# A streaming-encoder block on one core: the first two down products of each feed-forward add into the residual in HBM

## The chip, the core and the metric

The kernel runs on one core of a Trainium2 chip. The core has a matrix engine (TensorE, PE in the profile, with its weight loads shown apart as PEld), three engines for elementwise work (VectorE or DVE, ScalarE or ACT, GpSimd or POOL), SyncE (SP), which here only issues transfers, and 16 DMA engines that move data between HBM, on-chip SBUF and so on. Products land in PSUM. Each engine works through its own list of instructions in order and waits on semaphores of the others. The metric is the device time of one execution in microseconds (us), the median of several runs; less is better.

## What is computed

One layer of an encoder block on x of 256 rows by 2048 columns, fp32: a half-step feed-forward, a mixer (pooling and gated linear attention), cross-attention to 256 memory tokens, a second half-step feed-forward, and a last norm.

```python
def swiglu(h, w_gate, w_up, w_down):
    return (jax.nn.silu(h @ w_gate) * (h @ w_up)) @ w_down
...
x = x + 0.5 * swiglu(rms_norm(x, ffn1_norm[l]), ffn1_w_gate[l], ffn1_w_up[l], ffn1_w_down[l])
...
x = x + jnp.concatenate([y_pool, y_gla], axis=-1) @ w_out[l]
x = x + mem_cross_attention(rms_norm(x, xattn_norm[l]), rms_norm(mem, mem_norm[l]),
                            xattn_w_q[l], xattn_w_kv[l], xattn_w_o[l])
x = x + 0.5 * swiglu(rms_norm(x, ffn2_norm[l]), ffn2_w_gate[l], ffn2_w_up[l], ffn2_w_down[l])
```

The inner width of the feed-forward is 5632. All weights, some 400 MB, are read once.

## The kernel before

**Products.** Each fp32 operand is split into a high and a low half of TensorE's own fp32 type, and a product is three matmuls (high by high, high by low, low by high) of 128x512 results. The weights come in units of 1 MB (`raw`, three buffers). ACT makes the high half `wh` by a cast, VectorE the low half `wl` by a subtraction. A plain unit is 24 matmuls. Some units are done with seven products in place of eight (`split_seven`, `seven`): VectorE first adds weight pieces into a tile `T`, both `T` and three pieces of `raw` are split (`wh`, `wl`, `xh`, `xl`), and the unit is 21 matmuls. Sums of the activations for such units are made once (`Sums`).

**Units and blocks.** `Stream` holds a list of units and of small operations between them, and emits them in order: a unit's weights are split two units ahead of its products, and its load is issued three units ahead of that split. A scheduler then sets the final order on each engine. `block_s` does one block of eight units for 1024 output columns in four PSUM tiles: two `whole` tiles that all units use, and two `parts` tiles that only the seven-product units use. When the last seven-product unit is done, `combine` (L579) turns the parts into an SBUF tile `e` (tag `sg`, two buffers): one copy on ACT and three sums on VectorE. At the block's end `join` (L593) finishes each half of 512 columns.

**Two ways to finish a block.** Gate and up blocks pass no `merge`: `join` has VectorE add the whole tile to `e` (L598), and both `combine` and `join` are marked `clump`, so that the last 768 of 2048 columns of the low half of the unit split just ahead go to GpSimd (`low_parts`, L459), which runs it beside VectorE's sums. Down blocks go through `into_x` (L834): the residual rows `x` (1024 columns, 256 rows, also tag `sg`) are fetched from HBM by SP, `early_parts` (L776) adds both halves of `e` to them as soon as the parts are combined (L781, twice), `residual` (L765) adds the two whole tiles at the block's end (L769, twice), and SP stores the rows to the HBM tiles `X[0]` and `X[1]` (L763). The factor 0.5 of the half-step is the scalar of these additions.

**Feed-forward.** `ffn` (L859) cuts the inner width into three parts of 2048, 2048 and 1536 columns (`FF_PARTS`). A part is gate and up blocks, then a down of two blocks, one for each `X[b]`. The first two downs take `WHOLE` (L825), eight units a block. The third down of the first feed-forward also turns the updated rows for the next norm; the third of the second feed-forward ends the kernel (`down_end`). The first down of the first feed-forward fetches its rows from the input x. `finish_norm` (L299) makes the factor `Rcol` of each row, which the gate uses in ACT's Silu (L874) and the up in VectorE's product (L882).

Of the kernel before, what the change touches and what calls it, by code (L numbers as in the profile page):

```python
# [8 lines left out]
F32R = mybir.dt.float32r  # L9
# [90 lines left out]
def build(ctx, tc, I, out):  # L100
# [68 lines left out]
    def ctl(name, shape):  # L169
        return whole_lines(const, shape, F32, name, name)  # L170
# [9 lines left out]
    gains = ctl("gains", [P, G_END])  # L180
    Rcol = ctl("Rcol", [P, 2])
    Rm = ctl("Rm", [P, 2])
# [116 lines left out]
    def finish_norm(n, spread_too=True):  # L299

        nc.vector.tensor_reduce(out=sums, in_=ss[:, :, :n], axis=AX.X, op=ALU.add)
        done = rsqrt(Rcol, sums, D, 2)
        if spread_too:
            diag["R"] = [diagonal(Rcol[:, t : t + 1]) for t in range(2)]
        return done
# [100 lines left out]
    class Sums:  # L406
# [8 lines left out]
        def make(self, g):  # L415
            act, i = self.act, self.pairs.index(g)
            n = 3 if self.over else 4
            if self.own and (i == 0 or i >= self.room):
                room, tag = (self.room, self.name) if i == 0 else (1, f"{self.name}{i}")
                t = scope["pool"].tile([P, room * 6 * P], F32R, tag=tag, name=uid(tag))  # L420
# [413 lines left out]
    def into_x(w, act, scale, gain=None, k0=0, nk=KT, spread_too=True, src=None, way=OUTPUT,  # L834
# [13 lines left out]
        if gain is not None:  # L848
            st.op(lambda: finish_norm(4, spread_too), way.folds[3] + 1)
            if spread_too:  # L850
                st.op(spread_norm, spread_at)

    FF_PARTS = ((0, 4), (4, 4), (8, 3))

# [4 lines left out]
    def ffn(wg, wu, wd, down, amid=None, end=None):  # L859
# [19 lines left out]
        def ev_up(j, c, held=gate):  # L879
            g = held[j]  # L880
            for h in range(2):
                nc.vector.scalar_tensor_tensor(  # L882
                    out=g[:, h, :], in0=c[:, h, :], scalar=Rcol[:, h : h + 1], in1=g[:, h, :],
                    op0=ALU.mult, op1=ALU.mult,
                )
# [55 lines left out]

    st.op(lambda: among_weights(first_factor), 6)
    st.op(more_gains, 14)
    st.op(lambda: turn_gains(G_MIX, G_END), 35)
# [7 lines left out]
    def down_first(wd, k0, nk, last, way):  # L952
        way.make_sums()
        if last:
            for g, after in zip(qk_sums.pairs[:2], (9, 11)):
                st.op(lambda g=g: among_weights(lambda: qk_sums.make(g)), after)
        into_x(wd, ys, 0.5, G_MIX if last else None, k0, nk, src=None if k0 else I["x"][0],
               way=way, spread_at=7)

# [543 lines left out]
    def down_last(wd, k0, nk, last, way):  # L1503
        if last:
            down_end(wd, k0, nk, way)
        else:
            way.make_sums()
            into_x(wd, ys, 0.5, None, k0, nk, way=way)

# [9 lines left out]
    def down_end(wd, k0, nk, way):  # L1519
# [45 lines left out]
        def update(nb, h):  # L1565
            xn = x_cols(nb * NB, NB)[:, h]
            return nc.vector.scalar_tensor_tensor(
                out=xn, in0=acc_ps[nb][:, h, :], scalar=0.5, in1=xn, op0=ALU.mult, op1=ALU.add
            )
# [6 lines left out]
        def last_update(i):  # L1576
            xn = x_cols(3 * NB, NB)[:, 1, columns(i)]
            return nc.vector.scalar_tensor_tensor(
                out=xn, in0=last_part(i), scalar=0.5, in1=xn, op0=ALU.mult, op1=ALU.add
            )  # L1580
# [98 lines left out]
        for b in range(2):  # L1679
            into = lambda j, ps: acc_ps.__setitem__(2 + j, ps)  # L1680
            block_s(wwide(wd, b * 2 * NB, k0, nk - 2), ys, way.sums, END_ORDER[b],
                    into if b else residual(0.5, 0, None), early_parts(0.5, b), (0,),
                    home=end_parts(b), more=b == 1)
# [78 lines left out]
```

## Time and profile before

| | |
|---|---|
| median of 3 runs | 2071.29 us (2071.0 to 2071.98) |
| span of the profiled execution | 2069.6 us |
| busy PE, DVE, ACT, POOL | 2059.1, 1843.7, 1173.7, 103.5 us |
| DMA, mean over the span | 211 GB/s, 435.92 MB |
| SP queue | 122840 packets, 434.12 MB |
| first down of the first feed-forward | 178.1 to 264.3 us, two blocks |

The profile gives no time of the profiled execution beside its span, so the span is set against the median of the runs, which is 1.7 us longer. A group of instructions is a line with its engine, operation, tile names (written tile, arrow, tiles read), shape, count, busy time, mean time of one in ns, and the idle time before it with what ended it. A row of the timeline begins with its start in us and its time. A matmul of 512 columns is shown with about 0.39 us, but the next one starts some 0.23 us after it, since they are pipelined; what counts for PE is the distance between starts.

### The profile page before, as it was taken

To read this page: it belongs to the slowest core of one execution; us is meant where nothing else is said; L and a number is where in the kernel's file an instruction comes from. 1 tells how busy PE (TensorE), PEld (TensorE's weight loads), DVE (VectorE), ACT (ScalarE), POOL (GpSimd) and SP (SyncE) were. 2 spreads that over 40 slices of the span, in tenths; PEclk is the share of its full clock that TensorE was granted. 3 is DMA by queue.
4 is the path that set the end of the run, shared out by engine and by line. 5 is a ranking of instruction groups with operands and counts; after the bars stand their busy time and mean duration, and the time that the engine had idled before them with its cause. 6 is when DMAs were issued, how large, how long until landed. Compare 5 with 4: busy or idle time off the path is not lost.

```text
span 2069.6 us, 24068 instructions
## 1 busy us (share of the span) xinstructions
PE 2059.1 (99%) x9464; PEld 1714.5 (83%) x9464; DVE 1843.7 (89%) x1720; ACT 1173.7 (57%) x1196; POOL 103.5 (5%) x93
## 2 busy tenths in 40 slices
PE   9999999999999999999999999999999999999998
PEld 7888888888888888888888888888888888888886
DVE  7998899989998779989889787989988999889987
ACT  7654455554554666665765544656554565545554
POOL 0000000000000000000000000000000010000001
PEclk9999999999999999999999999999999999999999
DMA  7666766566666655467655455666577765676664
GB/s 265 205 202 224 243 214 215 184 227 238 225 202 224 226 184 183 163 205 280 225 185 192 159 178 183 203 224 224 171 235 225 239 208 185 225 241 224 210 224 156
DMA packets 123129, 435.92 MB, mean 211 GB/s; under 512 B 9860, under 2 KB 13544, under 8 KB 122632
## 3 DMA queue, kind: packets, MB, share of 16 engines
q1 hardware_dynamic: 122840, 434.12, 62.9%
q8 instruction: 74, 1.21, 0.2%
q14 instruction: 39, 0.32, 0.0%
q10 hardware_dynamic: 176, 0.27, 0.0%
HBM read 417.58 MB, written 16.78 MB: 210 GB/s over the span
## 4 chain that ended last, share of the span: by engine, by line
PE 99%; DMA 0%; DVE 0%; SPq 0%; ACT 0%; POOL 0%; POOLq 0%; issue 0%; DVEq 0%
PE pt L362 64%; PE pt L509 30%; PE ph L791 2%; PE pl L1416 1%; PE pv L1453 1%; PE px L802 1%; PE pp L1049 0%; DMA x<-in_x 0%; PE pa L1077 0%; PE tm L1362 0%; PE po L1215 0%; PE px L728 0%; PE pq L1202 0%; PE pe L362 0%; PE pz L1093 0%; PE po L1218 0%
## 5 line engine op out<-in xcount | busy, mean ns | idle before, releaser
L362 PE MATMUL pt<-wh,xs 128*128 128x512 f32 x2432 | 780.8, 391 | 0.0
L1720 ACT CAST wh<-raw 128x2048 fp32r<-128x2048 f32 x242 | 461.7, 1912 | 228.9 <-PE pt L362 128.0
L455 DVE TENSOR_TENSOR wl<-raw,wh 128x2048 fp32r<-128x2048 f32 (+1 forms) x242 | 515.9, 2140 | 83.9 <-ACT wh L1720 83.7
L362 PEld LDWEIGHTS pt<-wh,xs 128*128 128x128 f32 x2432 | 455.9, 188 | 94.1 <-issue 0.5
L491 ACT CAST wh<-T 128x1024 fp32r<-128x1024 f32 x264 | 277.0, 1054 | 379.0 <-DVE T L488 362.4
L362 PE MATMUL pt<-wl,xs 128*128 128x512 f32 x1216 | 474.0, 390 | 0.0
L362 PE MATMUL pt<-wh,ys 128*128 128x512 f32 x1452 | 458.1, 389 | 0.0
L362 PEld LDWEIGHTS pt<-wh,ys 128*128 128x128 f32 x1452 | 272.5, 188 | 56.1
L455 DVE TENSOR_TENSOR wl<-T,wh 128x2048 fp32r<-128x2048 f32 (+1 forms) x132 | 296.7, 2248 | 5.6 <-ACT wh L491 5.2
L362 PE MATMUL pt<-wl,ys 128*128 128x512 f32 x726 | 283.0, 390 | 0.0
L362 PEld LDWEIGHTS pt<-wl,xs 128*128 128x128 f32 x1216 | 228.4, 188 | 46.2
L280 DVE TENSOR_TENSOR xl<-raw,xh 128x1536 fp32r<-128x1536 f32 x132 | 231.1, 1751 | 10.8 <-ACT xh L279 10.7
L279 ACT CAST xh<-raw 128x1536 fp32r<-128x1536 f32 x132 | 195.5, 1481 | 52.1 <-PE pt L509 30.7
L488 DVE TENSOR_TENSOR T<-T,raw 128x512 f32<-128x512 f32 x264 | 182.0, 690 | 6.8
L488 DVE TENSOR_TENSOR T<-raw 128x1024 f32<-128x1024 f32 x132 | 160.7, 1218 | 0.6
L362 PEld LDWEIGHTS pt<-wl,ys 128*128 128x128 f32 x726 | 136.3, 188 | 28.1
L509 PE MATMUL pt<-xh,xs 128*128 128x512 f32 x416 | 154.9, 389 | 0.0
L509 PE MATMUL pt<-wh,xs 128*128 128x512 f32 x396 | 153.9, 389 | 0.0
L459 POOL TENSOR_TENSOR wl<-raw,wh 128x768 fp32r<-128x768 f32 x44 | 81.6, 1854 | 1389.6 <-DVE wl L455 1366.8
L509 PE MATMUL pt<-wh,xe 128*128 128x512 f32 x320 | 124.3, 389 | 0.0
L509 PEld LDWEIGHTS pt<-xh,xs 128*128 128x128 f32 x416 | 78.1, 188 | 16.2
L509 PEld LDWEIGHTS pt<-wh,xs 128*128 128x128 f32 x396 | 74.3, 188 | 15.4
(274 smaller groups left out, 2081.4 us busy)
## 6 DMA issues: line engine op xcount, KB each, us to landing
raw<-in_ffn_w_down SPq DMA_DIRECT2D x88, 1024.0 KB, 5.5
raw<-in_ffn_w_up SPq DMA_DIRECT2D x80, 1024.0 KB, 5.0
raw<-in_ffn_w_gate SPq DMA_DIRECT2D x77, 1024.0 KB, 5.1
raw<-in_w_in SPq DMA_DIRECT2D x32, 1024.0 KB, 5.0
raw<-in_xattn_w_kv SPq DMA_DIRECT2D x32, 1024.0 KB, 5.0
raw<-in_w_out SPq DMA_DIRECT2D x16, 1024.0 KB, 6.7
raw<-in_xattn_w_q SPq DMA_DIRECT2D x16, 1024.0 KB, 6.2
raw<-in_xattn_w_o SPq DMA_DIRECT2D x16, 1024.0 KB, 5.7
```

The lines of the kernel that those rows point to most:

```text
L279: in_turn("scalar", lambda: nc.scalar.copy(hi, src))
L280: in_turn("vector", lambda: nc.vector.tensor_tensor(out=lo, in0=src, in1=f32(hi), op=ALU.subtract))
L362: latest["product"] = nc.tensor.matmul(ps, a, w, start=first and i == 0, stop=last and i == 2)
L455: in_turn("vector", lambda: nc.vector.tensor_tensor(out=lo[:, :n], in0=src[:, :n], in1=f32(hi[:, :n]), op=ALU.subtract))
L459: rest = nc.gpsimd.tensor_tensor(out=lo[:, n:], in0=src[:, n:], in1=f32(hi[:, n:]), op=ALU.subtract)
L488: in_turn("vector", lambda: nc.vector.tensor_tensor(out=o, in0=a, in1=b, op=ALU.add))
L491: in_turn("scalar", lambda: nc.scalar.copy(th[:, c], t[:, c]))
L509: nc.tensor.matmul(banks[n], x, w, start=n in fresh and j == 0, stop=n in ends and j == 2)
L791: rows["turned"] = nc.tensor.transpose(v[:, i, h * P : (h + 1) * P], g[:, h, i * P : (i + 1) * P], ident)
L802: nc.tensor.transpose(v[:, j, h * P : (h + 1) * P], x[:, h, j * P : (j + 1) * P], ident)
L1416: nc.tensor.matmul(ps[:, t, :M], ys[:, 4 * h + d, a, tok], xa["K", h][:, d, b, :], start=i == 0, stop=i == 11,)
L1720: in_turn("scalar", lambda: nc.scalar.copy(hi, raw))
```

## The change

In the first two downs of each feed-forward the residual rows are no longer fetched to SBUF, added to on VectorE and stored. `onto_x` takes the place of `into_x`: its blocks have no `merge`, so they finish like gate and up blocks (join into `e` on VectorE, both steps marked `clump`), and then GpSimd issues two transfers a block that add the joined 256 x 512 halves of `e` to `X[b]` in HBM. For the first down `X` must hold x already: eight transfers from HBM to HBM, issued by SP, copy the input (`copy_x`). The half-step's 0.5 moves into the up factor (`Rup`, one more VectorE instruction in each norm), and the additions of the third downs get 1.0. `Sums.make` names another home for sums past its first tile; no sums of this kernel lie past it. The products are the same.

```diff
-    Rcol = ctl("Rcol", [P, 2])
+    factors = ctl("Rcol", [P, 4])
+    Rcol, Rup = factors[:, :2], factors[:, 2:]
...
-        done = rsqrt(Rcol, sums, D, 2)
+        rsqrt(Rcol, sums, D, 2)
+        done = nc.vector.tensor_scalar_mul(Rup, Rcol, 0.5)
...
+    def copy_x(i):
+
+        b, rows_i = i % 2, slice(i // 2 * S // 4, (i // 2 + 1) * S // 4)
+        nc.sync.dma_start(X[b][rows_i, :], I["x"][0][rows_i, b * 2 * NB : (b + 1) * 2 * NB])
+
+    def added_to_x(b):
+
+        def evict(j, e):
+            nc.gpsimd.dma_start(
+                X[b][:, j * NB : (j + 1) * NB].rearrange("(h p) n -> p h n", p=P), e,
+                accum_op=ALU.add,
+            )
+        return evict
+
+    def onto_x(w, act, k0, nk, way):
+
+        for b in range(2):
+            block_s(wwide(w, b * 2 * NB, k0, nk), act, way.sums, way.orders[b], added_to_x(b),
+                    sevens=way.sevens[b])
...
-                    out=g[:, h, :], in0=c[:, h, :], scalar=Rcol[:, h : h + 1], in1=g[:, h, :],
+                    out=g[:, h, :], in0=c[:, h, :], scalar=Rup[:, h : h + 1], in1=g[:, h, :],
...
+    for i in range(8):
+        st.op(lambda i=i: copy_x(i), 15 + 2 * i)
...
-        if last:
-            for g, after in zip(qk_sums.pairs[:2], (9, 11)):
-                st.op(lambda g=g: among_weights(lambda: qk_sums.make(g)), after)
-        into_x(wd, ys, 0.5, G_MIX if last else None, k0, nk, src=None if k0 else I["x"][0],
-               way=way, spread_at=7)
+        if not last:
+            onto_x(wd, ys, k0, nk, way)
+            return
+        for g, after in zip(qk_sums.pairs[:2], (9, 11)):
+            st.op(lambda g=g: among_weights(lambda: qk_sums.make(g)), after)
+        into_x(wd, ys, 1.0, G_MIX, k0, nk, way=way, spread_at=7)
...
-            into_x(wd, ys, 0.5, None, k0, nk, way=way)
+            onto_x(wd, ys, k0, nk, way)
```

The built programs show where the scheduler put these steps. In the rows below the line number is that of each kernel's own file, a number behind a tile's name tells its buffers apart, and nothing tells of times.

SP's list at the start, from the last column of gains to the loads of the weights of the first gate block (`raw_219` is the fifth load of the kernel). Before:

```order
L685 DMA gain_787<-in_gla_b_a 4x128
L638 DMA raw_219<-in_ffn_w_gate 128x2x1024
L638 DMA raw_228<-in_ffn_w_gate 128x2x1024
L638 DMA raw_283<-in_ffn_w_gate 128x2x1024
L638 DMA raw_336<-in_ffn_w_gate 128x2x1024
```

Now:

```order
L689 DMA gain_788<-in_gla_b_a 4x128
L860 DMA X_105<-in_x 64x1024
L860 DMA X_106<-in_x 64x1024
L642 DMA raw_219<-in_ffn_w_gate 128x2x1024
L860 DMA X_105<-in_x 64x1024
L860 DMA X_106<-in_x 64x1024
L860 DMA X_105<-in_x 64x1024
L860 DMA X_106<-in_x 64x1024
L642 DMA raw_228<-in_ffn_w_gate 128x2x1024
L860 DMA X_105<-in_x 64x1024
L860 DMA X_106<-in_x 64x1024
L642 DMA raw_283<-in_ffn_w_gate 128x2x1024
```

The code asks for the copies from the 15th unit on, but they wait for nothing, and the scheduler moved them up: two stand ahead of the fifth load, six ahead of the sixth and eight ahead of the seventh.

ACT's list where the first gate block ends and the first up block (the ninth load, `wh_505` before, `wh_506` now) begins; `sg_583<-pt_174` and `sg_584<-pt_174` are the Silu of the first gate bank. Before:

```order
L279 CAST xh_507<-raw_389 128x1536
L285 CAST xs<-j_494 128x128
L285 CAST xe_268<-j_494 128x384
L491 CAST wh_505<-T_504 128x1024 x2
L1720 CAST wh_543<-raw_395 128x2048
L874 ACTIVATE sg_583<-pt_174,Rcol 128x512 x2
```

Now:

```order
L280 CAST xh_508<-raw_389 128x1536
L286 CAST xs<-j_495 128x128
L286 CAST xe_268<-j_495 128x384
L495 CAST wh_506<-T_505 128x1024
L898 ACTIVATE sg_584<-pt_174,Rcol 128x512 x2
L495 CAST wh_506<-T_505 128x1024
L1747 CAST wh_544<-raw_395 128x2048
```

The Silu of the first bank now stands between the two casts of that load's high half.

VectorE's list where the first block of the first down ends (about 214 to 235 us in the profile). Before:

```order
L455 TENSOR_TENSOR wl_1701<-raw_1596,wh_1700 128x2048
L584 TENSOR_TENSOR sg_1727<-pt_1637,sg_1727 128x512
L585 TENSOR_TENSOR sg_1727<-pt_1638,sg_1727 128x1024
L455 TENSOR_TENSOR wl_1735<-raw_1635,wh_1734 128x2048
L488 TENSOR_TENSOR T_1768<-raw_1674 128x1024
L588 TENSOR_TENSOR sg_1727<-pt_1638,sg_1727 128x512
L781 SCALAR_TENSOR_TENSOR x_1547<-sg_1727,x_1547 128x2x512
L488 TENSOR_TENSOR T_1768<-T_1768,raw_1674 128x512
L781 SCALAR_TENSOR_TENSOR x_1547<-sg_1727,x_1547 128x2x512
L769 SCALAR_TENSOR_TENSOR x_1547<-pt_1458,x_1547 128x2x512
L488 TENSOR_TENSOR T_1768<-T_1768,raw_1674 128x512
L280 TENSOR_TENSOR xl_1772<-raw_1674,xh_1771 128x1536
```

Now:

```order
L459 TENSOR_TENSOR wl_1706<-raw_1601,wh_1705 128x1280
L588 TENSOR_TENSOR sg_1733<-pt_1642,sg_1733 128x512
L589 TENSOR_TENSOR sg_1733<-pt_1643,sg_1733 128x1024
L592 TENSOR_TENSOR sg_1733<-pt_1643,sg_1733 128x512
L459 TENSOR_TENSOR wl_1739<-raw_1640,wh_1738 128x1280
L602 TENSOR_TENSOR sg_1733<-pt_1466,sg_1733 128x1024
L602 TENSOR_TENSOR sg_1733<-pt_1467,sg_1733 128x1024
L492 TENSOR_TENSOR T_1773<-raw_1679 128x1024
L492 TENSOR_TENSOR T_1773<-T_1773,raw_1679 128x512 x2
L281 TENSOR_TENSOR xl_1777<-raw_1679,xh_1776 128x1536
L459 TENSOR_TENSOR wl_1775<-T_1773,wh_1774 128x2048
```

The four additions to `x_1547` are gone and two joins into `sg_1733` stand in their place, ahead of the sums of the next seven-product unit (`T_1773`) and no longer among them; both plain low halves next to the sums are 1280 columns long in place of 2048.

POOL's list at the same place, where before it held nothing from `wl_1416` of the first down's second unit to `wl_2220` of the next part's first gate block. Now:

```order
L463 TENSOR_TENSOR wl_1706<-raw_1601,wh_1705 128x768
L463 TENSOR_TENSOR wl_1739<-raw_1640,wh_1738 128x768
L865 DMA X_105<-sg_1733 128x2x512 x2
L463 TENSOR_TENSOR wl_1913<-raw_1818,wh_1912 128x768
L463 TENSOR_TENSOR wl_2015<-raw_1917,wh_2014 128x768
L865 DMA X_106<-sg_1940 128x2x512 x2
L463 TENSOR_TENSOR wl_2222<-raw_2132,wh_2221 128x768
```

Four shares of low halves and two transfers for each half of the residual are new; each pair of transfers stands behind the shares of its block's end.

More of the change, by code (lines that the diff above doesn't have):

```diff
@@ L418, in make @@
             if self.own and (i == 0 or i >= self.room):
-                room, tag = (self.room, self.name) if i == 0 else (1, f"{self.name}{i}")
-                t = scope["pool"].tile([P, room * 6 * P], F32R, tag=tag, name=uid(tag))
+                if i == 0:
+                    t = scope["pool"].tile([P, self.room * 6 * P], F32R, tag=self.name, name=uid(self.name))
+                else:
+                    t = scope["pool"].tile([P, 4 * NB], F32R, tag="sg", name=uid("sx"), bufs=2)
                 held = min(len(self.pairs), self.room) if i == 0 else 1
@@ L1567, in update @@
             return nc.vector.scalar_tensor_tensor(
-                out=xn, in0=acc_ps[nb][:, h, :], scalar=0.5, in1=xn, op0=ALU.mult, op1=ALU.add
+                out=xn, in0=acc_ps[nb][:, h, :], scalar=1.0, in1=xn, op0=ALU.mult, op1=ALU.add
             )
@@ L1578, in last_update @@
             return nc.vector.scalar_tensor_tensor(
-                out=xn, in0=last_part(i), scalar=0.5, in1=xn, op0=ALU.mult, op1=ALU.add
+                out=xn, in0=last_part(i), scalar=1.0, in1=xn, op0=ALU.mult, op1=ALU.add
             )
@@ L1681, in down_end @@
             block_s(wwide(wd, b * 2 * NB, k0, nk - 2), ys, way.sums, END_ORDER[b],
-                    into if b else residual(0.5, 0, None), early_parts(0.5, b), (0,),
+                    into if b else residual(1.0, 0, None), early_parts(1.0, b), (0,),
                     home=end_parts(b), more=b == 1)
```

## The prediction

> **What bounds the kernel now.** I read the busy shares first, then the chain that ended last, then the waits of TensorE alone, then the two blocks of the first down by windows.
>
> ```profile
> PE 2059.1 (99%) x9464; PEld 1714.5 (83%) x9464; DVE 1843.7 (89%) x1720; ACT 1173.7 (57%) x1196; POOL 103.5 (5%) x93
> PE 99%; DMA 0%; DVE 0%; SPq 0%; ACT 0%; POOL 0%; POOLq 0%; issue 0%; DVEq 0%
> PE pwarm L206 <- POOL ident masks.py:199: 1.4, 1, 1.4
> PE px L728 <- DMA x<-in_x: 0.5, 1, 0.5
> 178.10:222.30 44.20, 44.20 (x205) 36.80 (x204) 37.34 (x40) 23.21 (x20) 0.14 (x1) 1.00 0.61 214
> 222.30:264.30 42.00, 42.00 (x187) 34.79 (x186) 40.74 (x32) 21.09 (x16) 0.00 (x0) 1.00 0.73 243
> ```
>
> TensorE (PE) is busy 99% and is 99% of the chain. In the whole run it waits for another engine twice, 1.9 us together, both before its first product. The two windows are the first down's blocks (columns: length, then busy us of PE, PEld, DVE, ACT and POOL with counts, the granted clock, the share of the DMA engines, GB/s): PE fills both, at clock 1.00. A busy PE could still hide products that run late, but 42.00 us over 187 products is 0.225 us each, and the window from 54 to 90 us, quoted below, has 161 in 36.00, 0.224: one pace in both stages. So I find no stall in these blocks that could be given back. VectorE (DVE) is close behind, 40.74 of 42.00 in the second block: work taken from it becomes margin, not time.
>
> **The downs: VectorE's part.** Each of eight blocks (two downs in each of two feed-forwards, two blocks each) loses four additions to fetched rows and gains two joins.
>
> ```profile
> L769 DVE SCALAR_TENSOR_TENSOR x<-pt,x 128x1024 f32<-128x1024 f32 x30 | 36.1, 1215 | 0.0
> L781 DVE SCALAR_TENSOR_TENSOR x<-sg,x 128x1024 f32<-128x1024 f32 x26 | 31.4, 1216 | 0.0
> L598 DVE TENSOR_TENSOR sg<-pt,sg 128x1024 f32<-128x1024 f32 x52 | 62.2, 1217 | 5.8 <-PE pt L362 5.8
> L455 DVE TENSOR_TENSOR wl<-raw,wh x242: 1478/2284/2294, 22.6 to 2046.6; 128x2048 fp32r<-128x2048 f32 x102, 128x1280 fp32r<-128x1280 f32 x19
> L459 POOL TENSOR_TENSOR wl<-raw,wh x44: 1842/1853/1867, 95.2 to 1998.3; 128x768 fp32r<-128x768 f32 x44
> ```
>
> Four at 1.216 us against two at 1.217 leaves 2.43 us. The combine and the joins are now of the kind that hands 768 columns of a low half to GpSimd (POOL): 50 such shares become 65, two more per block less one in the first feed-forward, each 2.28 - 1.48 = 0.80 us off VectorE. So 2.43 + 1.60 = 4.0 us a block, 32 us in all. What that is worth is read at the end of the first block:
>
> ```profile
> 219.60 0.69 DVE L584 TENSOR_TENSOR sg<-pt,sg 128x512 f32<-128x512 f32 x1 [3.14 <-ACT sg L583]
> 220.39 1.23 DVE L585 TENSOR_TENSOR sg<-pt,sg 128x1024 f32<-128x1024 f32 x1
> ...
> 223.86 1.22 DVE L488 TENSOR_TENSOR T<-raw 128x1024 f32<-128x1024 f32 x1
> 224.99 0.68 DVE L588 TENSOR_TENSOR sg<-pt,sg 128x512 f32<-128x512 f32 x1
> ...
> 229.60 0.68 DVE L488 TENSOR_TENSOR T<-T,raw 128x512 f32<-128x512 f32 x1
> 230.20 1.75 DVE L280 TENSOR_TENSOR xl<-raw,xh 128x1536 fp32r<-128x1536 f32 x1
> ...
> 233.00 2.28 DVE L455 TENSOR_TENSOR wl<-T,wh 128x2048 fp32r<-128x2048 f32 x1
> ...
> 236.00 0.39 PE L509 MATMUL pt<-wl,ys 128*128 128x512 f32 x1
> ```
>
> The low half written at 233.00 is ready at 235.28 and read at 236.00: 0.7 us to spare, no stall. In the new order (quoted above) the combine still waits for ACT's copy of the same products, so it starts at 219.6 and its third sum ends at 222.3. Behind it stand the short low half (1.48, to 223.8), two joins (2.43, to 226.2), the three sums of T (1.22 + 0.68 + 0.68, to 228.8), the low half xl of 1.75 (230.5) and this one (232.8). The margin grows from 0.7 to 3.2 us, and the time does not move. POOL's part of the low half ends 1.85 after 223.8, and the joins end at 226.2; PE has the 24 products of the unit ahead to run from 222.3 (24 x 0.225, to 227.7), so the weights and the banks are there when it wants them. **Downs: 0.** If that cover went, a block would lose what its margin lacks, not more.
>
> One rule speaks against those shares.
>
> ```profile
> 1033.44 1.86 POOL L459 TENSOR_TENSOR wl<-raw,wh 128x768 fp32r<-128x768 f32 x1 [147.25 <-DVE wl L455]
> 1034.36 1.08 DVE L286 TENSOR_TENSOR xs<-j,xs 128x128 fp32r<-128x128 f32 x1
> ```
>
> This VectorE sum of two SBUF tensors, 0.29 us elsewhere, took 1.08 beside a share. The Trainium skill, "SBUF — State Buffer", Who interferes with whom, says that a VectorE instruction with two SBUF inputs contends with a GpSimd instruction that reads SBUF; the trace agrees with this 0.8 us. By that rule alone the 15 new shares would cost VectorE some 12 us, and by what follows none. Here a share (1.85) lies beside a combine (0.69 + 1.22 + 0.69) or two joins (2.43), which read one operand from PSUM, so I take 0; at 0.8 us each the two of a block would leave 2.4 of its 4.0 us.
>
> **The transfers.** The new rows on POOL wait for the joins; the next share behind them comes five units later or more, and the buffer that they read is wanted again by the next part's gate at the earliest. SP loses 16 fetches and 16 stores, 2 MB a block, and gets no wait in return. No row shows a transfer that adds. By the page all traffic costs
>
> ```profile
> q1 hardware_dynamic: 122840, 434.12, 62.9%
> ...
> raw<-in_ffn_w_down SPq DMA_DIRECT2D x88, 1024.0 KB, 5.5
> ```
>
> Packets, MB and share of the 16 engines stand in the first row: 0.629 x 2069.6 / 434.12 = 3.0 us of all 16 engines per MB. The 1 MB added in a block is bounded by 3.0 us (a plain move) and 9.0 (sum, old row and new row each counted), against 6.0 removed: -3 to +3 us of engines in some 42 us, where they are busy 0.61 to 0.73. I take a read and a write, 6.0, what goes in its place, so **0**. The cover is the time that a weight lies ready:
>
> ```profile
> 223.97 0.37 SPq L638 DMA_DIRECT2D raw<-in_ffn_w_down  x1
> 233.07 1.48 ACT L279 CAST xh<-raw 128x1536 fp32r<-128x1536 f32 x1
> ```
>
> It was issued at 223.97, landed by the median of 5.5 at 229.5 and was first read at 233.07, 3.6 us later.
>
> **The start.** The scheduler put the eight copies of x (2 MB) at 20 us, among the weights.
>
> ```profile
> 20.72 10.52 SPq L638 DMA_DIRECT2D raw<-in_ffn_w_gate  x4
> ...
> 20.00:22.00 2.00, 2.00 (x10) 1.68 (x9) 0.92 (x4) 1.82 (x4) 0.00 (x0) 1.00 0.29 29
> 22.00:32.00 10.00, 10.00 (x51) 8.28 (x51) 7.44 (x9) 7.09 (x12) 0.00 (x0) 1.00 0.84 311
> ...
> 29.18 1.91 ACT L1720 CAST wh<-raw 128x2048 fp32r<-128x2048 f32 x1
> ...
> 32.08 1.91 ACT L1720 CAST wh<-raw 128x2048 fp32r<-128x2048 f32 x1 [0.58 <-DMA raw<-in_ffn_w_gate]
> ...
> 33.06 4.49 DVE L455 TENSOR_TENSOR wl<-raw,wh 128x2048 fp32r<-128x2048 f32 x2
> ...
> 38.02 0.39 PE L362 MATMUL pt<-wl,xs 128*128 128x512 f32 x1
> ...
> 43.26 0.39 PE L362 MATMUL pt<-wl,xs 128*128 128x512 f32 x1
> ```
>
> Six copies stand ahead of the sixth weight load and eight ahead of the seventh. At 3.0 us per MB a copy takes 0.75 us of the engines, 4.5 and 6.0 us; the gap at 20 to 22 us (share 0.29) absorbs 1.4, so 3.1 and 4.6 later. The sixth cast then starts at 29.18 + 3.1 = 32.3 at the latest, its low half 1.9 later, ready at 36.5 for a read at 38.02. The seventh: 32.08 + 4.6 = 36.7, ready at 40.9 for 43.26. Both hold, 1.5 and 2.4 us to spare: **0**. If reading and writing HBM count twice (9.0 - 1.4 = 7.6 and 12.0 - 1.4 = 10.6 later), the sixth is ready at 41.0 and the seventh at 46.9: a stall of up to 3.6 us. I take the single price, that of the row.
>
> Behind it ACT now evicts the first gate bank between the two casts of the ninth load's high half.
>
> ```profile
> 50.88 1.05 ACT L491 CAST wh<-T 128x1024 fp32r<-128x1024 f32 x1 [0.89 <-DVE T L488]
> 52.43 2.28 DVE L455 TENSOR_TENSOR wl<-T,wh 128x2048 fp32r<-128x2048 f32 x1
> 53.66 1.25 ACT L874 ACTIVATE sg<-pt,Rcol 128x512 f32<-128x512 f32 x2
> 55.04 0.39 PE L509 MATMUL pt<-wl,xs 128*128 128x512 f32 x1
> 54.00:90.00 36.00, 36.00 (x161) 29.80 (x160) 35.58 (x32) 23.20 (x23) 0.00 (x0) 1.00 0.68 229
> 78.79 2.28 DVE L455 TENSOR_TENSOR wl<-T,wh 128x2048 fp32r<-128x2048 f32 x1
> 82.02 0.39 PE L509 MATMUL pt<-wl,xs 128*128 128x512 f32 x1
> ```
>
> The second cast ends at 51.93 + 1.25 = 53.2 or a little later, and VectorE's low half moves by 0.8 to 1.3 us, to 55.5 or 56.0; PE reads it four products later than before (ninth, not fifth), near 55.95. VectorE stays late, because it is busy 35.58 of the next 36.00 us, and the smallest margin there is 82.02 - 81.07 = 0.95. **Stall 0 to 0.4; I take 0.3.** The factor of a half, one small VectorE instruction in each norm, adds under 0.2 us to that lateness and lies within it.
>
> **Sum.** 2069.6 + 0 + 0 + 0.3 = 2069.9 us of span. The runs' median, 2071.29, stands 1.7 above the span, so 2071.6.
>
> **Rivals.**
> 1. *Copies at twice the price*: 3.6 us of stall at 37 to 47 us, 2075. For: DMA is busy 0.84 of 22 to 32 us, and the seventh cast waits for its weights already. Against: the casts have 1.5 and 2.4 us to spare.
> 2. *The sums starve the weights* (slower). They take turns with the weight loads on the same engines. At their upper price a load comes up to 9.0 us late; its 3.6 us before the cast and PE's 3.2 cover 6.8, and eight blocks lose 2.2 us each: 2089. It decides from about 7 us per MB. Against: 2 MB in the same 42 us stall nothing now. Beside it, the Trainium skill, "DMA: Bandwidth & Descriptors", Issuing engines are not separate DMA queues, says that transfers of all engines run on the same 16; no run here shows a sum yet.
> 3. *VectorE's 32 us come back* (faster): hidden lateness of 0.3 us goes in each block and the 1.9 us of waits with it, 2067. Against: the windows, and the two PE waits.
> 4. *The change does less than it says*: if VectorE's additions went but the transfers were hidden worse, this is rival 2; if nothing moved, 2071.3, inside the forecast.
>
> **How the numbers follow.** A difference of 0.2%, 4.1 us, is about what a measurement of this kernel can tell from no change. Forecast 0.70; rival 1, 0.17, of which a quarter passes 4.1 us; rival 2, 0.10; rival 3, 0.03. Faster 0.03, same 0.83, slower 0.14. The range goes from 2070.0 (1.3 us of hidden lateness recovered) over the forecast and rival 1 up to 2077 (rival 1 and a little of rival 2); outside lie most of rival 2 and rival 3, 0.13.
>
> **What would show it.** PE still at 99%, with no wait row against a weight's low half beyond tenths of a us; DVE busy near 1843.7 - 32 = 1812 us; POOL near 103.5 + 15 x 1.85 = 131 us and its queue's transfers. Right at the start: the sixth and seventh casts move to 32 and 37 us with PE at full pace. Wrong: gaps between products at 37 to 47 us (rival 1), or in each down with casts that wait for in_ffn_w_down (rival 2).

## The result, and the profile after

The changed kernel takes 2074.86 us (median of 20 runs, 2073.93 to 2077.09) against 2071.61 us for the kernel before in the same rounds (20 runs, 2070.83 to 2072.4). The ratio is 1.0016, with a 95% interval of 1.001 to 1.0023: 3.25 us slower. That is inside the range of the prediction and under its 0.2%, but it is not the forecast of +0.3 us; it is close to what rival 1 gave. Of the runs below, one execution of `third_both` took 2965 us at a granted clock of 0.65 and is left out of its median.

Busy shares, the chain that ended last, and what TensorE waited for (us in total, times, longest), of the kernel after:

```profile
PE 2060.7 (99%) x9464; PEld 1713.7 (83%) x9464; DVE 1817.9 (88%) x1708; ACT 1174.3 (57%) x1196; POOL 149.9 (7%) x124
PE 97%; DMA 2%; DVE 1%; ACT 0%; SPq 0%; issue 0%; POOL 0%; POOLq 0%; DVEq 0%; ACTq 0%
PE pwarm L207 <- POOL ident masks.py:199: 1.4, 1, 1.4
PE pt L364 <- DVE wl L459: 1.2, 1, 1.2
PE px L732 <- DMA x<-in_x: 0.6, 1, 0.6
PE pt L513 <- DVE wl L459: 0.2, 1, 0.2
```

VectorE lost 25.8 us of work and TensorE gained nothing from it. Two waits for a low half are new, 1.4 us together, and the chain now holds 2% of DMA. Both belong to the start of the program, which shows best when one compares the start of the same product, counted from the first, in the two traces (both kernels have 9464 products in PE's list).

| product | start before, us | after, later by |
|---|---|---|
| 30th | 8.7 | 0.29 |
| 143rd | 31.9 | 0.29 |
| 145th | 32.3 | 1.71 |
| 246th | 54.8 | 1.69 |
| 252nd | 56.2 | 2.21 |
| 371st | 83.1 | 2.54 |
| 551st | 123.9 | 3.08 |
| last | 2060.8 | 3.12 |

The first 0.29 us is not the change's: in the other kernels below this start-up lies between -0.65 and +1.69 us. Then 1.42 us are lost between two products at 32 us, 0.52 between 55 and 56 us, 0.87 bit by bit until 124 us, and 0.04 in all the rest, which holds all eight changed blocks. The two windows of the first down show the same thing (columns as in the prediction):

```profile
178.00:222.00 44.00, 44.00 (x204) 36.57 (x203) 36.51 (x39) 19.99 (x17) 3.69 (x2) 1.00 0.55 191
222.00:264.00 42.00, 42.00 (x187) 34.79 (x186) 36.24 (x28) 22.71 (x17) 6.20 (x4) 1.00 0.76 236
```

PE fills both at clock 1.00, with as many products in the second block as before (187); VectorE's 40.74 us there became 36.24.

The 32 us place first in the kernel before: the cast of the fifth load's high half, its low half, and the first product that reads the low half.

```profile
26.62 1.90 ACT L1720 CAST wh<-raw 128x2048 fp32r<-128x2048 f32 x1
...
28.55 2.29 DVE L455 TENSOR_TENSOR wl<-raw,wh 128x2048 fp32r<-128x2048 f32 x1 [1.28 <-ACT wh L1720]
...
32.09 0.40 PE L362 MATMUL pt<-wl,xs 128*128 128x512 f32 x1
```

The low half is ready at 30.84 and read at 32.09: 1.25 us of margin, where the sixth load has 38.02 - 35.35 = 2.7. After, with SP's issues around it:

```profile
20.90 1.23 SPq L860 DMA_DIRECT2D X<-in_x  x2
22.24 0.53 SPq L642 DMA_DIRECT2D raw<-in_ffn_w_gate  x1
22.82 3.22 SPq L860 DMA_DIRECT2D X<-in_x  x4
26.14 0.55 SPq L642 DMA_DIRECT2D raw<-in_ffn_w_gate  x1
29.41 1.91 ACT L1747 CAST wh<-raw 128x2048 fp32r<-128x2048 f32 x1 [2.39 <-DMA raw<-in_ffn_w_gate]
29.45 4.59 SPq L642 DMA_DIRECT2D raw<-in_ffn_w_gate  x2
31.35 2.29 DVE L459 TENSOR_TENSOR wl<-raw,wh 128x2048 fp32r<-128x2048 f32 x1 [3.79 <-ACT wh L1747]
33.69 0.50 PE L364 MATMUL pt<-wl,xs 128*128 128x512 f32 x1 [1.16 <-DVE wl L459]
34.47 1.91 ACT L1747 CAST wh<-raw 128x2048 fp32r<-128x2048 f32 x1 [0.91 <-DMA raw<-in_ffn_w_gate]
38.94 1.91 ACT L1747 CAST wh<-raw 128x2048 fp32r<-128x2048 f32 x1 [1.59 <-DMA raw<-in_ffn_w_gate]
```

The fifth load is issued at 22.24 in place of 20.72, and its cast waits for it until 29.41, 2.8 us later than before (0.3 of this is the start's). The low half follows; 1.25 us are margin, and TensorE stands for the rest. The sixth and seventh casts come at 34.47 and 38.94 and TensorE does not wait for them. The chain through this stretch of the kernel after (start, us, what) shows how the transfers hang together:

```profile
12.07 8.82 DMA raw<-in_ffn_w_gate
...
22.24 7.15 DMA raw<-in_ffn_w_gate
...
29.45 9.47 DMA raw<-in_ffn_w_gate
```

The copies' issue waits until the fourth load has landed, two issues of 0.6 us go ahead of the fifth load, and the seventh is issued at 29.45 only, when the fifth has landed. In the traces of both kernels, at the start, SP's transfers use eight semaphores in turn, and each transfer waits until the one eight places ahead of it on SP's list has landed. The first copy stands eight places behind the fourth load, as the fifth load does in the kernel before; and with the sixth load and six copies between them, the seventh load now stands eight places behind the fifth. In the kernel before it was issued at 24.95, ahead of the fifth's landing at 25.72. So a copy takes a place in this row even where its bytes do no harm.

The new transfers and the queue that carries them (packets, MB, share of 16 engines), and GpSimd's groups:

```profile
q0 software_dynamic: 4352, 8.39, 2.3%
...
raw<-in_ffn_w_down SPq DMA_DIRECT2D x88, 1024.0 KB, 5.5
X<-sg POOLq DMA_DIRECT2D x16, 512.0 KB, 10.0
...
L463 POOL TENSOR_TENSOR wl<-raw,wh 128x768 fp32r<-128x768 f32 x60 | 111.0, 1849 | 1433.7 <-DVE wl L459 1410.9
L865 POOL DMA_DIRECT2D X<-sg x16 | 19.4, 1324 | 1.7 <-DVE sg L602 1.7
```

0.023 x 2072.9 / 8.39 = 5.7 us of 16 engines per MB, and the loads of the down's weights land after 5.5 us as before.

### The profile page after: what moved, and what is told of

Its sections match the earlier page's. It is cut to its first block, busy times and chain, and to the rows that moved or that the text cites. A ratio compares the mean times of both kernels' runs of the same rounds, so it can differ in the third digit from the quotient of the medians.

```text
span 2072.9 us, 24083 instructions
## 1 busy us (share of the span) xinstructions
PE 2060.7 (99%) x9464; PEld 1713.7 (83%) x9464; DVE 1817.9 (88%) x1708; ACT 1174.3 (57%) x1196; POOL 149.9 (7%) x124
## 3 DMA queue, kind: packets, MB, share of 16 engines
q0 software_dynamic: 4352, 8.39, 2.3%
## 4 chain that ended last, share of the span: by engine, by line
PE 97%; DMA 2%; DVE 1%; ACT 0%; SPq 0%; issue 0%; POOL 0%; POOLq 0%; DVEq 0%; ACTq 0%
PE pt L364 62%; PE pt L513 30%; PE ph L795 2%; DMA raw<-in_ffn_w_gate 1%; PE pl L1443 1%; PE pv L1480 1%; PE px L806 1%; DMA x<-in_x 0%; PE pp L1076 0%; DVE wl L459 0%; PE pa L1104 0%; PE tm L1389 0%; PE po L1242 0%; PE pq L1229 0%; SPq L642 0%
## 5 line engine op out<-in xcount | busy, mean ns | idle before, releaser
L459 DVE TENSOR_TENSOR wl<-raw,wh 128x2048 fp32r<-128x2048 f32 (+1 forms) x242 | 503.4, 2088 | 98.8 <-ACT wh L1747 98.7
L364 PEld LDWEIGHTS pt<-wh,xs 128*128 128x128 f32 x2432 | 455.9, 188 | 94.2 <-issue 0.5
L364 PEld LDWEIGHTS pt<-wh,ys 128*128 128x128 f32 x1452 | 272.4, 188 | 56.2
L463 POOL TENSOR_TENSOR wl<-raw,wh 128x768 fp32r<-128x768 f32 x60 | 111.0, 1849 | 1433.7 <-DVE wl L459 1410.9
L492 DVE TENSOR_TENSOR T<-raw 128x1024 f32<-128x1024 f32 x132 | 160.9, 1219 | 0.6
L602 DVE TENSOR_TENSOR sg<-pt,sg 128x1024 f32<-128x1024 f32 x68 | 81.4, 1219 | 9.1 <-PE pt L364 9.0
```

The costliest lines, as they stand in the source:

```text
L364: latest["product"] = nc.tensor.matmul(ps, a, w, start=first and i == 0, stop=last and i == 2)
L459: in_turn("vector", lambda: nc.vector.tensor_tensor(out=lo[:, :n], in0=src[:, :n], in1=f32(hi[:, :n]), op=ALU.subtract))
L463: rest = nc.gpsimd.tensor_tensor(out=lo[:, n:], in0=src[:, n:], in1=f32(hi[:, n:]), op=ALU.subtract)
L492: in_turn("vector", lambda: nc.vector.tensor_tensor(out=o, in0=a, in1=b, op=ALU.add))
L602: among_weights(lambda: (None, nc.vector.tensor_tensor(out=e, in0=held["ps"][j], in1=e, op=ALU.add if j else ALU.subtract)))
```

## The experiments

After the result the question was which part costs the 3.1 us, in three theories. A: the copies of x, through the fifth load and what VectorE does later because of it. B: the copies only at 32 us; the factor `Rup` and ACT's order for the rest. C: the adding transfers.

### The copies moved, the copies alone, the factor alone

`in_order` is the changed kernel with the copies pinned behind the loads that they are written behind:

```diff
-        nc.sync.dma_start(X[b][rows_i, :], I["x"][0][rows_i, b * 2 * NB : (b + 1) * 2 * NB])
+        tc.keep_in_program_order(nc.sync.dma_start(
+            X[b][rows_i, :], I["x"][0][rows_i, b * 2 * NB : (b + 1) * 2 * NB]))
```

> The changed kernel with its eight copies of x pinned on SP behind the loads they are written behind (one every other weight load, from the 20th load on), instead of ahead of the fifth. Nothing else changes. In the changed kernel's trace its products stand 1.6 us later than before's at 34 us, 2.1 at 58 us, 3.0 at 126 us and 3.1 at the end. Theory A (the copies hold up the fifth load, and the lateness of VectorE up to 126 us follows from that): 2071.3 to 2072.0 us, no wait of PE for the low half near 33 us, 0.6 us or less behind before at 126 us. Theory B (only the 1.4 us stall is the copies'; the 1.5 us between 56 and 126 us come from the new factor and ACT's order at the ninth load): 2073.1. Theory C (the adding transfers cost it): 2074.8, unchanged.

Measured: 2072.33 us against 2071.59, ratio 1.0003 (0.9994 to 1.0012). The interval holds 1, so the traces must decide. Its products stand 0.66 us ahead of before's at 32 us, 0.06 ahead at 56 us, and 0.07 ahead at the end. The wait at 33 us is gone. This agrees with A for 32 us and for the bits up to 124 us, which go to nothing, and leaves the ninth load: 0.60 us between 55 and 56 us, for which the time is 0.3 us above A's range. C is out.

`before_copies` is the kernel before with only this:

```diff
+    for i in range(8):
+        st.op(lambda i=i: copy_x(i), 15 + 2 * i)
```

> The kernel before with the eight copies alone, at the places where the changed kernel has them (two ahead of the fifth load, six ahead of the sixth, eight ahead of the seventh); the first down overwrites what they write. Theory A: 2074.2 to 2074.9 us, a wait of PE for the fifth load's low half of 1.2 to 1.4 us near 33 us and 2.5 to 3.1 us behind before at 126 us. Theory B: 2073.0, the stall alone. Theory C: 2071.6.

Measured: 2074.28 us, ratio 1.0013 (1.0004 to 1.0022), 2.7 us slower. 1.28 us are lost at 32 us, 0.13 at 55 us, 0.85 up to 124 us, 0.05 after it. A again: B expected no loss after the stall.

`before_rup` is the kernel before with the factor alone:

```diff
-        done = rsqrt(Rcol, sums, D, 2)
+        rsqrt(Rcol, sums, D, 2)
+        done = nc.vector.tensor_scalar_mul(Rup, Rcol, 0.5)
```

> The kernel before with the new factor alone (one small VectorE instruction in each norm; nothing reads it), which also puts one of the two Silu of the first gate bank between ACT's two casts of the ninth load. Theory A: 2071.3 to 2072.0 us, at most 0.5 us of stall at the ninth load. Theory B: 2073.1, with 1.5 us of stalls between 54 and 126 us. Theory C: 2071.6.

Measured: 2072.12 us, ratio 1.0003 (0.9994 to 1.0012). 0.60 us are lost at the ninth load, a little more than A's 0.5, and nothing elsewhere. So the factor costs 0.6, not the 1.5 of B; by the times alone this is not told from no change. The two parts alone are 2.7 and 0.5 us slower, 3.2 together, against 3.25 for the whole change.

### What about a copy delays the fifth load

`before_small` is `before_copies` with 128 of the 1024 columns in each copy: as many issues and rows, an eighth of the bytes.

```diff
-        nc.sync.dma_start(X[b][rows_i, :], I["x"][0][rows_i, b * 2 * NB : (b + 1) * 2 * NB])
+        nc.sync.dma_start(X[b][rows_i, : NB // 4], I["x"][0][rows_i, b * 2 * NB : b * 2 * NB + NB // 4])
```

> As the kernel before with the copies alone, but each copy moves 128 of its 1024 columns: as many issues and rows, an eighth of the bytes. If SP's time to issue is what delays the fifth load: it is issued at 22.2 us as in the changed kernel, its cast starts near 28 us, the stall of PE is 0.3 us or more and the run takes 2072 to 2073 us. If the bytes on the engines are: the cast starts at 26.6 to 27.2 us and the run takes 2071.3 to 2071.9 us.

Its rows at the start:

```profile
20.66 1.23 SPq L856 DMA_DIRECT2D X<-in_x  x2
21.99 0.53 SPq L638 DMA_DIRECT2D raw<-in_ffn_w_gate  x1
27.18 1.91 ACT L1727 CAST wh<-raw 128x2048 fp32r<-128x2048 f32 x1 [0.87 <-DMA raw<-in_ffn_w_gate]
```

2071.69 us, ratio 1.0002 (0.9993 to 1.0011); nothing is lost at 32 us. The two issues put the load back by 1.3 us on the clock, much as in the changed kernel, but the cast starts only 0.6 us later than before, 1.0 counted against its own products, which are 0.4 ahead. In the changed kernel that is 2.5, so some 1.5 us are the bytes, and without them the margin of 1.25 us holds. The ninth load costs 0.60 us here too, though VectorE has no factor to make and ACT runs both casts ahead of the Silu, as in the kernel before: the seventh load is issued at 27.21, when the fifth has landed, in place of 24.95, and the late loads put VectorE 0.7 us behind its products (the table further down). The bits up to 124 us are missing.

Are they the bytes ahead of the load or those behind it? `two_ahead` leaves only the two copies ahead of the fifth load at the start, `six_behind` only the other six, behind it:

```diff
+        if i >= 2:
+            tc.keep_in_program_order(copy)
```

```diff
+        if i < 2:
+            tc.keep_in_program_order(copy())
+        else:
+            with tc.issue_after(fifth[0].ins):
+                copy()
```

> The changed kernel with the two copies ahead of the fifth load left there and the other six pinned in program order (from the 20th load on). In the changed kernel the fifth load is issued at 22.24 us in place of 20.72, its cast starts at 29.41 in place of 26.62 and PE waits 1.2 us. If what stands ahead of the fifth load on SP delays it (0.5 MB and two issues): the cast again starts near 29.4 us and PE waits about 1.2 us; 2073.5 us or more. If the four copies behind it, which share the engines with it, do the larger part: the cast starts at 27 to 28 us, PE waits 0.4 us or less, and the time is 2072.0 to 2072.8.

> The counterpart: the fifth load keeps its place, four copies follow it and two the sixth load, and the first two are pinned in program order. If only what stands ahead counts: the fifth cast starts at 26.6 us, no wait of PE, 2072 to 2072.6 us. If the copies behind it share the engines with it: the cast starts at 28 us or later, PE waits 0.3 us or more, and the time is 2073 to 2074.5. The part of the sum that one of the two kernels shows and the other does not is then the split of the 2.8 us by which the cast came late.

Rows and a window of `two_ahead`, then the same window of the kernel before (the last two columns are the share of the DMA engines and GB/s), then the fifth to seventh casts of `six_behind`:

```profile
22.19 12.34 SPq L642 DMA_DIRECT2D raw<-in_ffn_w_gate  x4
29.90 1.91 ACT L1749 CAST wh<-raw 128x2048 fp32r<-128x2048 f32 x1 [3.03 <-DMA raw<-in_ffn_w_gate]
24.00:26.00 2.00, 2.00 (x12) 1.68 (x11) 1.97 (x3) 0.22 (x1) 0.00 (x0) 1.00 0.66 164
```

```profile
24.00:26.00 2.00, 2.00 (x13) 1.65 (x12) 1.78 (x3) 0.18 (x2) 0.00 (x0) 1.00 1.03 422
```

```profile
27.12 1.90 ACT L1756 CAST wh<-raw 128x2048 fp32r<-128x2048 f32 x1
31.89 1.92 ACT L1756 CAST wh<-raw 128x2048 fp32r<-128x2048 f32 x1 [1.71 <-DMA raw<-in_ffn_w_gate]
36.72 3.71 ACT L1756 CAST wh<-raw 128x2048 fp32r<-128x2048 f32 x2
```

`two_ahead` (2075.04 us, ratio 1.0016, 1.0006 to 1.0025) has the whole stall, 1.87 us between the 143rd and the 145th product: two copies of 256 KB ahead are enough, and the four behind are not needed for it. The fifth load lands 7.7 us after its issue; in the kernel before it takes 5.0, and behind the small copies 5.2. The windows show 164 GB/s in place of 422, but not the same part of the load: in `two_ahead` 22 to 24 us move 244 GB/s, which is about the copies' 0.5 MB, and the load seems to begin behind them, while in the kernel before it began at 21 us, and 22 to 24 us moved 272 GB/s. `six_behind` (2074.14 us, ratio 1.0012, 1.0003 to 1.0021) has no wait at 32 us. There the sixth and seventh casts come late, 2.7 and 4.6 us after the 29.18 and 32.08 of the kernel before (0.5 is the start's); TensorE doesn't wait for those loads, but VectorE falls behind, and 2.1 us are lost between 54 and 56 us, 1.5 of them in waits for VectorE's halves (`in_order` loses 0.6 there without any copy at the start). So my either-or was wrong: copies ahead of the fifth load delay that load, copies behind it delay the later loads and with them VectorE, which pays at the ninth load. In the window of `six_behind` from 24 to 26 us, with four copies issued, the engines move 422 GB/s as well, so a copy beside a load doesn't by itself slow the engines. Why a load that begins behind copies takes 2 to 3 us longer to land isn't shown by these runs.

### The adding transfers

In `sums_twice` and `sums_plain` each of the sixteen is issued twice, or writes without adding; both start from `in_order`.

```diff
+            for _ in range(2):
```

```diff
-                accum_op=ALU.add,
```

> As the kernel with the copies in order, but each adding transfer is issued twice, so X gets the first two downs' products twice. In the changed kernel's trace the 8.39 MB that GpSimd issues take 2.3% of 16 engines in 2072.9 us, 5.7 us per MB; a block would now have 11.4 us of it instead of 5.7. If the transfers are hidden because the engines have room (share 0.55 and 0.76 in the first down's blocks): 2072.3 us and no wait in the downs. If they already stand near the point from which they starve the weights (rival 2 of the prediction put it at 7 us a block): up to 11.4 - 6.8 = 4.6 us a block, 2072.3 + 37 = 2109, with casts that wait for in_ffn_w_down.

> As the kernel with the copies in order, but GpSimd's transfers write the joined halves in place of adding them, so the residual of the first two downs is left out. It measures what the addition costs a transfer: if a sum costs as much as a write, the queue's share stays at 2.3% and the landing at 10 us; if it costs a read more, the share falls to 1.2 to 1.6% and the landing to 5 to 7 us. Time by either: 2072.3 us, since no transfer of a down is waited for.

The queue of `sums_twice`, its second block, and the queue and landing of `sums_plain`:

```profile
q0 software_dynamic: 8704, 16.78, 4.5%
222.00:264.00 42.00, 42.00 (x187) 34.80 (x186) 36.18 (x29) 22.26 (x17) 8.61 (x6) 1.00 0.84 248
```

```profile
q0 software_dynamic: 2304, 8.39, 1.1%
X<-sg POOLq DMA_DIRECT2D x16, 512.0 KB, 8.4
```

One execution each, 2072.33 and 2073.39 us. From the 30th product on, both lose the 0.6 us at the ninth load and no more than 0.03 us until the end. An addition takes 5.6 us of the engines per MB and a plain write 2.7, about half; twice the additions still fit, with the engines busy 0.84. The additions move the same 8.39 MB in 4352 packets, the plain writes in 2304: in the traces a packet of 2 KB that adds takes 187 ns, and a plain one of 4 KB 178 ns. The landing of a plain write fell to 8.4 us only (10.6 in `in_order`), not to the 5 to 7 that I expected.

### Is VectorE's margin worth something?

`third_seven` starts from `in_order` and makes a third unit of each second block one with seven products; the activations' sum for it uses the buffer that the fetched rows held.

```diff
-    WHOLE = IntoX((0, 4), (2, 5), ((1, 2, 3, 5, 0, 6, 4, 7), (1, 2, 0, 3, 4, 5, 6, 7)),
-                  ((0, 4), (0, 4)))
+    WHOLE = IntoX((0, 4, 6), (2, 5, 9), ((1, 2, 3, 5, 0, 6, 4, 7), (1, 2, 0, 3, 4, 5, 6, 7)),
+                  ((0, 4), (0, 4, 6)))
```

> The kernel with the copies in order, and a third unit with seven products (pair 6) in the second block of each of the four first two downs; its sum of activations lives in a buffer of the tag sg that the fetched rows held before. It takes 3 products of 0.227 us off TensorE in 4 blocks, 2.7 us, and costs VectorE some 4.3 us a block and 2.5 us a down. If the 4.0 us a block freed on VectorE are real margin: 2072.3 - 2.7 = 2069.6 us. If VectorE has no room for it in the second block (36.24 busy of 42.00 in the changed kernel): it stalls there by up to 1 us a block and the time is 2072 to 2074.

Measured: 2069.49 us against 2071.66, ratio 0.999 (0.9981 to 0.9999). The second block of the first down, of this kernel:

```profile
222.00:264.00 42.00, 42.00 (x187) 34.79 (x186) 41.34 (x39) 24.12 (x21) 6.22 (x4) 1.00 0.76 230
```

VectorE is busy 41.34 of 42.00 us, 5.1 more than the 36.24 of the changed kernel, and TensorE doesn't wait. The kernel before wasn't tried with such a unit; its 40.74 us and these 5.1 would not fit in 42.00.

`third_both` does it in the first blocks too, in the second blocks' order, with the sums made after 0, 2 and 5 units.

> As before, with the third such unit in both blocks of the four downs: 8 x 0.68 = 5.4 us off TensorE, 2072.3 - 5.4 = 2066.9 us if VectorE keeps up. It now costs VectorE 2 x 4.3 + 2.5 = 11.1 us a down, against the 8.0 that the change freed; blocks have 41.3 us each and VectorE was busy 36.5 and 36.24 us in them, so it would be full (98 to 100%), and stalls of 1 us a block would take half the gain back: 2070.

2078.16 us, ratio 1.0032 (1.0019 to 1.0044): slower than either, and far from the 2067 to 2070 expected. What TensorE waits for:

```profile
PE pt L513 <- ACT sx L286: 1.7, 4, 0.4
PE pt L513 <- ACT ys L286: 1.3, 4, 0.5
PE pt L513 <- DVE xl L281: 0.2, 1, 0.2
```

In the first blocks of the four downs the gaps between products add up to 2.2 to 2.7 us, in `in_order` to 0.1 or 0.2; two such units save 1.36 us a down. TensorE waits there for the sums of the activations (the rows of ACT), each once a down: they come too late for their first reader. The three rows make 3.2 of the some 10 us lost; the other gaps in these blocks have no row of their own, and what causes them is open. Another order of the first block wasn't tried.

`third_pool` is `third_seven` with the factor made on GpSimd, which puts ACT's two casts of the ninth load together again, and takes an instruction off VectorE:

```diff
-        rsqrt(Rcol, sums, D, 2)
-        done = nc.vector.tensor_scalar_mul(Rup, Rcol, 0.5)
+        done = rsqrt(Rcol, sums, D, 2)
+        nc.gpsimd.tensor_scalar_mul(Rup, Rcol, 0.5)
```

> The kernel with the third seven-product unit in the second blocks (2069.49 us), with the new factor made on GpSimd in place of VectorE; ACT's list at the ninth load is then that of the kernel before, both casts ahead of the Silu. If the 0.44 us that the products lose at the ninth load (in the kernel before with the factor alone, and in the kernel with the copies in order) come from the order of ACT there: 2069.0 us and no wait of PE near 56 us. If not: 2069.5.

2069.0 us against 2071.59, ratio 0.9987 (0.9978 to 0.9996), with no wait of PE near 56 us. (The 0.44 in the expectation is the 0.60 above.) It beats both kernels: the kernel before by 2.6 us in the same rounds, and the changed kernel by about 5.9, which was measured in other rounds.

The time came out as expected, but it doesn't show that ACT's order was the cause, since VectorE's list changed as well. The traces decide. Here is VectorE ahead of the ninth load's low half, first in the kernel before, then in `before_rup`, then in `before_copies` (the low half alone):

```profile
47.63 1.22 DVE L488 TENSOR_TENSOR T<-raw 128x1024 f32<-128x1024 f32 x1
48.76 0.29 DVE L286 TENSOR_TENSOR xs<-j,xs 128x128 fp32r<-128x128 f32 x1
```

```profile
48.88 0.29 DVE L287 TENSOR_TENSOR xs<-j,xs 128x128 fp32r<-128x128 f32 x1 [0.56 <-ACT xs L286]
...
52.23 1.75 DVE L281 TENSOR_TENSOR xl<-raw,xh 128x1536 fp32r<-128x1536 f32 x1
53.90 2.28 DVE L457 TENSOR_TENSOR wl<-T,wh 128x2048 fp32r<-128x2048 f32 x1
```

```profile
55.63 2.29 DVE L455 TENSOR_TENSOR wl<-T,wh 128x2048 fp32r<-128x2048 f32 x1 [0.92 <-ACT wh L491]
```

In `before_rup` nothing holds up the low half: VectorE goes to it straight from `xl`. It is late because the factor adds 0.20 us, and because `xs` now stands ahead of the sums of `T` and waits 0.56 us there for ACT. Only in `before_copies` does the low half wait for ACT's second cast. The lateness of the low half against the kernel's own products, and what TensorE loses at the ninth load:

| kernel | low half starts, us | products later than before's by | low half late by | lost |
|---|---|---|---|---|
| before | 52.43 | 0 | 0 | 0 |
| `third_pool` | 52.24 | -0.19 | 0.00 | 0 |
| `before_rup` | 53.90 | 0.74 | 0.73 | 0.60 |
| `in_order` | 52.51 | -0.65 | 0.73 | 0.60 |
| `before_small` | 52.73 | -0.42 | 0.72 | 0.60 |
| `six_behind` | 55.22 | 0.50 | 2.29 | 2.13 |
| `before_copies` | 55.63 | 2.01 | 1.19 | 0.13 |
| after | 55.70 | 1.69 | 1.58 | 0.52 |

The low half of the kernel before is ready at 54.71 and read at 55.04, a margin of 0.33 us. In the last two rows TensorE reads it four products later, which is 0.9 us more, so it loses little there, and some 1.1 us of VectorE's lateness are left: the 0.85 and 0.87 us that are lost bit by bit until 124 us.

## Why the prediction was right or wrong

- **Downs, 0: right.** 0.04 us over eight blocks and everything between them. VectorE's work became margin: in the second block 40.74 fell to 36.24 us, and `third_seven` used it. The groups of additions, joins and low halves moved by 31 us together, about as worked out; the busy time of the page fell by 25.8, not 32. The times of all VectorE instructions together fell by 29.0 us (1933.3 to 1904.3), and they overlap their neighbours by 3.2 us less (89.6 and 86.4 us above the busy time).
- **The rule on VectorE beside GpSimd:** by it 15 shares would have cost VectorE 12 us. The sums of two SBUF tensors kept their mean, T from T and raw 690 and now 691 ns over 264 of them, and the joins that the shares lie beside 1217 and now 1219 ns, as the prediction took it.
- **The transfers, 6.0 us of the engines per MB, and 0 of the time: right.** 5.7 measured. Rival 2 is out: with twice as many, 11 us a block, nothing is waited for. Its point of decision, 7 us, was too low; it let all of a block's transfers fall on one load, which no trace shows.
- **The start, 0: wrong, and this is the step that failed.** The text tested the sixth and seventh loads. The fifth, with two copies ahead of it, was left out, though its margin of 1.25 us was the smallest of the three. The working would have passed it too: two copies at 0.75 us less the 1.4 us that "the gap at 20 to 22 us absorbs" leave 0.1. That credit doesn't exist. In it SP waits for the fourth load to land, the copies as well as the fifth load, and in the kernel after the engines are busy 0.06 of it:

```profile
20.00:22.00 2.00, 2.00 (x11) 1.65 (x10) 1.16 (x5) 1.84 (x5) 0.00 (x0) 1.00 0.06 14
```

Then SP needs 1.3 us for two issues, and the load takes 7.15 us to land in place of 5.0. The sixth and seventh casts came 2.2 us later than forecast (34.47 for 32.3, 38.94 for 36.7), and their margins did hold at TensorE. What they cost was VectorE's time, which TensorE lost later, in part at the ninth load and in part in the 0.87 us up to 124 us; of this the prediction had seen only that "VectorE stays late". It priced the copies' bytes alone and left out their places on SP's list, by which the seventh load waited for the fifth to land.
- **Rival 1 had the time for a partly wrong reason.** 2075 was near, but its stall was to come from the sixth and seventh loads at 37 to 47 us by a double price for bytes; it came at 33 us from the fifth, and less than half of the 3.25 us is that stall. That the range reached up to this rival is why the measured time lies inside it; the agreement with 2075 is luck.
- **The ninth load, 0.3 (0 to 0.4): the size was near, the mechanism was another.** It lost 0.52 us here and 0.60 in the kernels without the large copies. The prediction put it down to the Silu between ACT's casts; by the table above VectorE itself comes late, through the factor's 0.20 us, its wait of 0.55 us for ACT's `xs`, and in the changed kernel the late loads. The prediction's "under 0.2 us" for the factor is the instruction alone; it left out that VectorE's list changes with it. That ACT's second cast would have held up the low half nearly as long here (it ends at 55.56, and the low half starts at 55.70) is why the figure came close. The read four products later was right.
- **POOL, 131 us: short by 19.** A transfer's issue counts as 1.32 us of GpSimd, 16 of them as 19.4 us of busy time; nobody waits for it.

## What to carry to other kernels

When a transfer is put among loads, take every load from there on, the first one behind it above all, and set its margin (from the end of its last split to the first read) against the whole delay, issue time on the queue's engine included; an idle stretch of the engines is no credit if the queue is waiting in it. Count places too: where a transfer waits for the one eight places ahead, every small transfer shortens the reach of the loads behind it. This scheduler moved transfers ahead that needed no data, so pin such a transfer where there is room. When one instruction is added, read the whole lists of the engines around it: here its neighbours' new order cost more than it did. Time taken off an engine that isn't the bound is worth nothing until work of the bounding engine is moved onto it: here 2072.33 to 2069.49 us with four units (each from its own rounds).

## What the runs showed of the hardware

- **Once TensorE's clock was halved after a pause of 1.6 us.** `two_ahead` waits until 34.19 us; the windows behind it (the third figure from the end is the granted clock):

```profile
PE pt L364 <- DVE wl L459: 1.6, 1, 1.6
...
34.00:36.00 2.00, 1.81 (x6) 1.44 (x7) 1.90 (x6) 1.79 (x4) 0.00 (x0) 0.71 0.45 68
36.00:38.00 2.00, 2.00 (x6) 1.63 (x5) 1.97 (x3) 2.00 (x6) 0.00 (x0) 0.50 0.95 385
38.00:40.00 2.00, 2.00 (x9) 1.59 (x9) 2.00 (x2) 0.68 (x3) 0.00 (x0) 0.94 0.64 121
```

It cost another 1.6 us (2.21 behind at the 145th product, 3.82 at the 161st); this execution is the slowest of its ten, so the others may not have had it. The 1.2 us of the changed kernel at the same place left the clock at 1.00, and so did a wait of 2.3 us near 8 us in `third_both`. The Trainium skill, "TensorE: Matmul & The Clock Gate", Why this matters for your kernels, gives about 3 us of idleness as the limit; here half of that was once too much. In the clock records of this trace the half clock lasts 3.41 us (34.84 to 38.26), and the full clock before and after it 27.31 and 2030.93 us, 8 and 595 times as long. If the clock is decided per such stretch, the pause of `two_ahead` lies whole in one, and that of `third_both`, which has a border at 8.70 us, falls apart into 0.75 and 1.54 us. This is argued from two traces, not shown.

- **Adding in HBM costs the engines about twice a plain write**, 5.6 to 5.7 us per MB against 2.7, in packets of half the size (2 KB against 4 KB) that take about as long each (187 against 178 ns), and lands 2.2 us later (10.6 us in `in_order` against 8.4 in `sums_plain`).
- **A load behind two copies of 256 KB from HBM to HBM landed later**: 7.15 and 7.7 us after its issue (changed kernel, `two_ahead`), where it took 5.0 in the kernel before and 5.2 behind copies of an eighth of the bytes; the first copies landed 3.5 and 3.9 us after their issue in `two_ahead`.
